# Two loops of a diffusion trunk: ScalarE copies each projection out of PSUM, VectorE works on the copies

## The chip, the cores and the metric

One NeuronCore of a Trainium2 chip runs the whole program. The metric is the device time of one execution in microseconds (us). Five engines work side by side: TensorE (PE, with its weight loads as PEld), VectorE (DVE), ScalarE (ACT), GpSimd (POOL) and SyncE (SP, which here only issues DMAs). Matrix products are written to PSUM; everything else lives in SBUF.

## The reference, cut to what matters

The program is one inference step of a trunk with two layers over 640 tokens (128 of context, 512 of latents) and a model width of 1024. In each layer four mixers run, and their outputs are gated, projected and merged. What the change touches is the end of a layer, in which the last branch's projection is merged and the output projection is added to the residual with a per-channel gate:

```
merged = pv + (1 + ttd) * (branch @ w_branch_out)   # last branch, per channel tile
x      = x + gate * (merged @ w_out)                # gate: one number per channel, one for latents, one for context
```

Here `pv` is the sum of the other three branches and `ttd` what the merge gate (a sigmoid, made from a tanh) needs for that branch; an earlier part of the kernel left both in device memory. After the second layer a last RMSNorm ends the trunk. All is float32.

## The kernel before, in words

Activations lie feature-major: a tile is 128 channels by 640 tokens, and the model width is 8 such tiles (`KD`). A float32 product is made of three TensorE products: each operand is split into a high part (a rounded copy, `hi`) and what is left (`lo = x - hi`), and `mm3` (lines 144 to 152) multiplies hi by hi (L148), weights' hi by activations' lo (L150) and weights' lo by activations' hi (L152). `split_to` (L128 to L131) makes the parts: ScalarE copies (L130), VectorE or POOL subtracts (L131). `w_chunk` (L133) loads a chunk of weights of 128 x 512 (`wraw`, by a DMA that SP issues) and splits it into `whi` and `wlo`; all three have two buffers. `fm_tile` (L154) makes one output tile: it takes a PSUM tile (tag `s`, two buffers), and for each chunk of weights runs four `mm3`.

Two loops at a layer's end are changed.

The **last branch's projection** (weights `wbo[l, 1]`, 8 tiles, one chunk each, 24 matmuls each). For each tile the PSUM result `bo` (traced as `s`) is read by VectorE in L1467, `ht = (ht + 1) * bo`, where `ht` has been loaded from `ttd`; L1468 adds `pv` (traced as `sq`), and `split_to` makes `hhi` and `hlo` (ScalarE L130, VectorE L131), which are the operands of the next loop. The split of the weights runs on ScalarE (`whi`) and POOL (`wlo`), as the last argument `G` says.

The **output projection** (weights `wout`, 8 tiles, two chunks each, 48 matmuls each). VectorE reads the PSUM result in L1477, twice a tile: once for the 512 latent tokens (a strided view of 2 x 256) and once for the 128 context tokens, since the gate `ga` differs, and adds the residual `xo` (also traced as `ht`). Then ScalarE squares the new tile and VectorE adds up the squares (`square_sum`, L252 to L261); in the last layer ScalarE also scales the tile by the last norm's weights.

In layer 0 both loops also carry steps of the next layer's state-space preparation: `preps(n)` takes `n` steps of a generator (tables `WPREPS` and `PREPS`, a number of steps for each tile). Its products `WY` and `WYt` come from VectorE (L462, and L464, which adds the two) and POOL (L463; later in the loop L513, L516 and L519 in the same manner); TensorE transposes the result (L449), ScalarE takes the transposes out of PSUM (L450, `Wt`) and issues the DMA that stores them (L452). In layer 1 there is nothing to prepare, and both loops stand alone.

TensorE runs its instructions in the order in which the code is written (`manual_schedule`). On the other engines, and on the DMA queues, a scheduler of the framework sets the order at build time, from the dependences and its own costs. So a change of the code can move instructions that it doesn't name.

Of the kernel before, what the change touches and what calls it, by code (L numbers as in the profile page):

```python
# [14 lines left out]
AF = mybir.ActivationFunctionType  # L15
ALU = mybir.AluOpType
AX = mybir.AxisListType

P = 128
# [3 lines left out]
NT = 640  # L23
# [32 lines left out]
def hybrid_kernel(ctx: ExitStack, tc: tile.TileContext, A, O, dbg=None):  # L56
    nc = tc.nc
    V, S, G, T = nc.vector, nc.scalar, nc.gpsimd, nc.tensor
# [12 lines left out]
    def taker(pool):  # L71
        def take(tag, shape, bufs=1, dt=F32):
            return pool.tile(shape, dt, tag=tag, name=nm(tag), bufs=bufs)
        return take
# [6 lines left out]
    def load(dst, src):  # L81
        nc.sync.dma_start(dst, src)
        return dst
# [44 lines left out]
    def split_to(hi, lo, src, eng=V):  # L128

        S.activation(hi, src, AF.Copy)  # L130
        eng.tensor_tensor(lo, src, f(hi), ALU.subtract)  # L131
# [22 lines left out]
    def fm_tile(src, mhi, mlo, nk=KD, eng=V):  # L154

        o = psum2()
        kc = min(nk, 4)
        for kq in range(nk // kc):
            w = w_chunk(src[kq], [P, kc, P], eng)
            for kk in range(kc):  # L160
                k = kq * kc + kk
                mm3([o[:, 0, 192:512], o[:, 1, 0:320]], w[0][:, kk], w[1][:, kk],
                    [mhi[:, k, 0:HF], mhi[:, k, HF:NT]], [mlo[:, k, 0:HF], mlo[:, k, HF:NT]], k == 0, k == nk - 1)
        return run2(o)[:, 192:832]
# [87 lines left out]
    def square_sum(at, acc, x, k, tag="sq", bufs=2, last=None):  # L252

        if k == 0:
            S.activation(acc, x, AF.Square)
        else:
            sq = at(tag, [P, NT], bufs)
            S.activation(sq, x, AF.Square)
            if k == last:
                return sq  # L260
            V.tensor_tensor(acc, acc, sq, ALU.add)  # L261
# [1025 lines left out]
    xat = taker(xp)  # L1287
    xt = xat("xt", [P, KD, NT])
# [5 lines left out]
    def preps(n):  # L1294

        for _ in range(n):
            next(prep, None)
# [4 lines left out]
    for l in range(DEPTH):  # L1302
# [10 lines left out]
        for k in range(KD):  # L1313
            sh, sc = mods[l, 0], mods[l, 1]
            t = xat("ht", [P, NT], 2)
# [137 lines left out]
        ga = mods[l, 2]  # L1453
# [5 lines left out]
        xat = taker(xp)  # L1459
# [3 lines left out]
        for d_ in range(KD):  # L1463
            bo = fm_tile(A["wbo"][l, 1, d_], *b, 4, G)
            t = load(xat("ht", [P, NT], 2), ttd[l][1][d_])
            pv = load(xat("sq", [P, NT], 2), mgd[l][2][d_])
            V.scalar_tensor_tensor(t, t, 1.0, bo, op0=ALU.add, op1=ALU.mult)  # L1467
            V.tensor_tensor(t, t, pv, ALU.add)  # L1468
            split_to(mhi[:, d_], mlo[:, d_], t)
            preps(WPREPS[d_])  # L1470
        xt = xat("xt", [P, KD, NT])
        acc = xat("acc", [P, NT])
        for d_ in range(KD):
            g = fm_tile(A["wout"][l, d_], mhi, mlo, KD, G)
            xo = load(xat("ht", [P, NT], 2), (A["xT"] if l == 0 else xd)[:, d_])
            for s_, v_ in ((0, samp), (1, lambda z: z[:, 256:384])):
                V.scalar_tensor_tensor(v_(xt[:, d_]), v_(g), ga[:, d_, s_:s_ + 1], v_(xo), op0=ALU.mult, op1=ALU.add)  # L1477
            if not last:
                nc.sync.dma_start(xd[:, d_], xt[:, d_])
            sq = square_sum(xat, acc, xt[:, d_], d_, last=KD - 1)  # L1480
            parts = [acc, sq]
            if last:
                S.activation(xt[:, d_], xt[:, d_], AF.Copy, scale=fnc[:, d_:d_ + 1])
            preps(PREPS[d_])
# [166 lines left out]
```

## Time and profile before

| | |
|---|---|
| median of 3 runs | 2310.57 us (2305.61 to 2311.26) |
| the profiled execution | 2309.3 us |
| its span | 2307.5 us |
| mean granted clock of TensorE | 0.961 |
| TensorE matmul busy | 2109.0 us, 91% |
| VectorE busy | 1375.3 us, 60% |
| ScalarE busy | 1031.0 us, 45% |
| POOL busy | 905.1 us, 39% |

Busy time is the time in which an engine runs an instruction, and the share is of the span. The span lies inside the execution's own time: here 1.8 us lie around it. These are averages over stages of different kinds, so they don't tell what limits the two loops; the rows further down are from those loops. They run twice: in layer 0 the first loop spans about 1115 to 1161 us and the second to 1238 us, in layer 1 the first spans about 2205 to 2234 us and the second to 2290 us.

### The profile page before, as it was taken

What the parts mean: (1) busy time and instruction counts of PE and PEld (TensorE: products, weight loads), DVE (VectorE), ACT (ScalarE), POOL (GpSimd) and SP (SyncE); (2) the same over time, 40 slices, a digit from 0 to 9 for tenths busy, and PEclk for the clock granted to TensorE, in tenths of its full rate; (3) what the DMA queues carried; (4) which work ended last, traced back from release to release, by engine and by line L of the source; (5) the groups of instructions that cost most, each with busy time, mean ns of one, the idle gap of its engine ahead of it and who ended that gap; (6) DMA issues with size and microseconds to landing.
All of it is one profiled execution on the core that took longest, in us unless ns stands there. A gap on an engine that the chain in (4) does not pass through costs nothing. (4 is left out here: it accounts for less than half of the span.)

```text
span 2307.5 us, 38266 instructions
## 1 busy us (share of the span) xinstructions
PE 2109.0 (91%) x14197; PEld 2010.3 (87%) x14197; DVE 1375.3 (60%) x2515; ACT 1031.0 (45%) x2069; POOL 905.1 (39%) x637
## 2 busy tenths in 40 slices
PE   5876889969999999998799999997999999999997
PEld 2876789969998889998788999897899899999997
DVE  7998672755455455665777685349345455565542
ACT  5332343314556665553233444341346656554332
POOL 4477431312335552345553364232132523234522
PEclk9988999989999999999899999998999999999998
DMA  6455576533745666666473386763384455566643
GB/s 219 118 189 200 183 240 189 175 90 120 214 140 152 179 193 181 182 196 198 155 252 129 117 249 217 248 180 93 102 249 131 148 149 156 174 188 184 201 148 116
DMA packets 238635, 400.60 MB, mean 174 GB/s; under 512 B 36400, under 2 KB 110128, under 8 KB 238448
## 3 DMA queue, kind: packets, MB, share of 16 engines
q1 hardware_dynamic: 224208, 372.13, 53.5%
q10 hardware_dynamic: 14240, 26.02, 3.1%
q8 instruction: 111, 1.82, 0.4%
q14 instruction: 76, 0.62, 0.1%
HBM read 279.67 MB, written 117.87 MB: 172 GB/s over the span
## 5 line engine op out<-in xcount | busy, mean ns | idle before, releaser
L131 POOL TENSOR_TENSOR flo<-fraw,fhi 128x512 fp32r<-128x512 f32 x368 | 528.4, 1443 | 897.4 <-ACT fhi L130 850.4
L148 PE MATMUL mm<-hhi,fhi 128*128 128x320 f32 x2048 | 667.2, 326 | 25.2 <-DVE gt L764 7.5
L152 PE MATMUL mm<-hhi,flo 128*128 128x320 f32 x2048 | 640.8, 313 | 7.0 <-POOL flo L131 7.0
L150 PE MATMUL mm<-hlo,fhi 128*128 128x320 f32 x2048 | 639.8, 312 | 0.0
L148 PEld LDWEIGHTS mm<-hhi,fhi 128*128 128x128 f32 x2048 | 393.7, 192 | 38.3 <-ACT rx L942 8.0
L152 PEld LDWEIGHTS mm<-hhi,flo 128*128 128x128 f32 x2048 | 391.2, 191 | 8.2 <-POOL flo L131 8.0
L150 PEld LDWEIGHTS mm<-hlo,fhi 128*128 128x128 f32 x2048 | 392.9, 192 | 0.8
L130 ACT ACTIVATE fhi<-fraw 128x512 fp32r<-128x512 f32 x368 | 228.2, 628 | 166.3 <-PE mm L150 102.7
L131 DVE TENSOR_TENSOR ptl<-sm,pth 128x512 fp32r<-128x512 f32 (+1 forms) x240 | 142.4, 621 | 166.0 <-ACT pth L130 165.7
L786 DVE TENSOR_REDUCE mx<-s 128x1 f32<-128x640 f32 (+1 forms) x240 | 167.4, 714 | 106.2 <-PE s L819 51.2
L131 POOL TENSOR_TENSOR wlo<-wraw,whi 128x512 fp32r<-128x512 f32 (+1 forms) x80 | 117.7, 1474 | 219.9 <-ACT whi L130 205.6
L130 ACT ACTIVATE pth<-sm 128x512 fp32r<-128x512 f32 (+1 forms) x240 | 122.2, 543 | 126.7 <-PE sm L846 97.6
L819 PE MATMUL s<-k,q 128*128 128x384 f32 (+5 forms) x1008 | 159.1, 305 | 2.6 <-ACT p L788 1.8
L819 PEld LDWEIGHTS s<-k,q 128*128 128x128 f32 (+1 forms) x1008 | 155.0, 189 | 3.5 <-ACT p L788 2.1
L130 ACT ACTIVATE whi<-wraw 128x512 fp32r<-128x512 f32 (+1 forms) x96 | 59.1, 617 | 168.1 <-PE s L150 88.2
L148 PE MATMUL mm<-bh,fhi 128*128 128x320 f32 x384 | 126.2, 329 | 5.5 <-DVE gt L764 3.6
L717 ACT ACTIVATE gt<-mm 128x320 f32<-128x320 f32 x192 | 83.0, 432 | 90.4 <-PE mm L152 88.7
L846 PE MATMUL sm<-ident,p 128*128 128x128 f32 x800 | 116.0, 274 | 7.9 <-DVE ptl L131 2.9
L869 PE MATMUL sm<-pth,v 128*128 128x256 f32 (+1 forms) x528 | 120.4, 282 | 0.3 <-ACT pth L130 0.3
L152 PE MATMUL mm<-bh,flo 128*128 128x320 f32 x384 | 119.8, 312 | 0.0
L150 PE MATMUL mm<-bl,fhi 128*128 128x320 f32 x384 | 119.8, 312 | 0.1
L869 PE MATMUL sm<-ptl,v 128*128 128x256 f32 (+1 forms) x440 | 112.6, 281 | 0.5 <-DVE ptl L131 0.5
(425 smaller groups left out, 4170.7 us busy)
## 6 DMA issues: line engine op xcount, KB each, us to landing
fraw<-in_wmerge SPq DMA_DIRECT2D x128, 256.0 KB, 3.0
fraw<-in_wgate SPq DMA_DIRECT2D x64, 256.0 KB, 2.9
fraw<-in_wmod SPq DMA_DIRECT2D x64, 256.0 KB, 2.8
mgd<-gt SPq DMA_DIRECT2D x48, 320.0 KB, 2.8
fraw<-in_wbo SPq DMA_DIRECT2D x48, 256.0 KB, 3.0
k<-dkd SPq DMA_DIRECT2D x64, 192.0 KB, 4.0
gtd<-gt SPq DMA_DIRECT2D x32, 320.0 KB, 3.3
pv<-mgd SPq DMA_DIRECT2D x32, 320.0 KB, 3.8
```

Source lines behind the costliest of these rows:

```text
L130: S.activation(hi, src, AF.Copy)
L131: eng.tensor_tensor(lo, src, f(hi), ALU.subtract)
L148: T.matmul(outs[i], lhsT=whi, rhs=mhis[i], start=first, stop=False)
L150: T.matmul(outs[i], lhsT=whi, rhs=mlos[i], start=False, stop=False)
L152: T.matmul(outs[i], lhsT=wlo, rhs=mhis[i], start=False, stop=last)
L717: S.activation(t[:, r[0]], r[1], AF.Tanh, scale=0.5)
L786: V.tensor_reduce(mx[:, 0:1], s, axis=AX.X, op=ALU.max, negate=True)
L819: T.matmul(o, lhsT=tok(q, t), rhs=k[:, a:b], start=i == 0, stop=i == n - 1)
L846: T.transpose(pt[:, a:a + P], p[:, jj, P * kt:P * kt + P], ident)
L869: T.matmul(o, lhsT=v, rhs=p_, start=n == 0, stop=n == len(todo) - 1)
```

## The change

In the first loop a new tile `ob` (128 x 640, two buffers) takes ScalarE's copy of the PSUM result, and VectorE's instruction reads `ob` in its place. In the second loop ScalarE multiplies the PSUM result by the gate while it copies (one instruction for the latents' view, one for the context), and VectorE adds the residual to the copy in one instruction over all 640 tokens, where there were two.

```diff
@@ -1464,7 +1464,9 @@
             bo = fm_tile(A["wbo"][l, 1, d_], *b, 4, G)
             t = load(xat("ht", [P, NT], 2), ttd[l][1][d_])
             pv = load(xat("sq", [P, NT], 2), mgd[l][2][d_])
-            V.scalar_tensor_tensor(t, t, 1.0, bo, op0=ALU.add, op1=ALU.mult)
+            ob = xat("ob", [P, NT], 2)
+            S.activation(ob, bo, AF.Copy)
+            V.scalar_tensor_tensor(t, t, 1.0, ob, op0=ALU.add, op1=ALU.mult)
             V.tensor_tensor(t, t, pv, ALU.add)
             split_to(mhi[:, d_], mlo[:, d_], t)
             preps(WPREPS[d_])
@@ -1473,8 +1475,10 @@
         for d_ in range(KD):
             g = fm_tile(A["wout"][l, d_], mhi, mlo, KD, G)
             xo = load(xat("ht", [P, NT], 2), (A["xT"] if l == 0 else xd)[:, d_])
+            ob = xat("ob", [P, NT], 2)
             for s_, v_ in ((0, samp), (1, lambda z: z[:, 256:384])):
-                V.scalar_tensor_tensor(v_(xt[:, d_]), v_(g), ga[:, d_, s_:s_ + 1], v_(xo), op0=ALU.mult, op1=ALU.add)
+                S.activation(v_(ob), v_(g), AF.Copy, scale=ga[:, d_, s_:s_ + 1])
+            V.tensor_tensor(xt[:, d_], ob, xo, ALU.add)
             if not last:
                 nc.sync.dma_start(xd[:, d_], xt[:, d_])
             sq = square_sum(xat, acc, xt[:, d_], d_, last=KD - 1)
```

In the changed kernel the copy of the first loop is line 1468, VectorE's two instructions are lines 1469 and 1470, the gated copies of the second loop are line 1480 and the addition is line 1481.

The scheduler places the new instructions, and moves others. Three places matter.

ScalarE in layer 1's first loop, before (`whi` is a weight chunk's high part, `hhi` a merged tile's high part):

```order
L130 ACTIVATE whi_24410<-wraw_24408 128x512
L130 ACTIVATE hhi_24286<-ht_24360 128x640
L130 ACTIVATE whi_24449<-wraw_24447 128x512
L130 ACTIVATE hhi_24286<-ht_24399 128x640
L130 ACTIVATE whi_24488<-wraw_24486 128x512
```

And in the changed kernel:

```order
L130 ACTIVATE whi_24407<-wraw_24405 128x512
L1468 ACTIVATE ob_24357<-s_24322 128x640
L130 ACTIVATE hhi_24318<-ht_24353 128x640
L130 ACTIVATE whi_24448<-wraw_24446 128x512
L1468 ACTIVATE ob_24398<-s_24363 128x640
L130 ACTIVATE hhi_24318<-ht_24394 128x640
L130 ACTIVATE whi_24489<-wraw_24487 128x512
```

The copy `ob` of a tile now stands between the weights' split for the tile two further on and the `hhi` of the same tile, which is made of what VectorE computes from that `ob`.

POOL in layer 0's first loop, before (`WYt` belongs to the preparation of the next layer, `wlo` is the low part of a weight chunk, here of tiles 2, 3 and 4 in that order):

```order
L463 TENSOR_TENSOR WYt_12565<-PW_6653,BX_12335 128x1024
L131 TENSOR_TENSOR wlo_12351<-wraw_12348,whi_12350 128x512
L463 TENSOR_TENSOR WYt_12692<-PW_6653,BX_12335 128x1024
L131 TENSOR_TENSOR wlo_12393<-wraw_12390,whi_12392 128x512
L463 TENSOR_TENSOR WYt_12711<-PW_6653,BX_12335 128x1024
L131 TENSOR_TENSOR wlo_12443<-wraw_12440,whi_12442 128x512
```

And in the changed kernel:

```order
L463 TENSOR_TENSOR WYt_12579<-PW_6653,BX_12339 128x1024
L131 TENSOR_TENSOR wlo_12355<-wraw_12352,whi_12354 128x512
L463 TENSOR_TENSOR WYt_12710<-PW_6653,BX_12339 128x1024
L463 TENSOR_TENSOR WYt_12729<-PW_6653,BX_12339 128x1024
L131 TENSOR_TENSOR wlo_12399<-wraw_12396,whi_12398 128x512
L131 TENSOR_TENSOR wlo_12451<-wraw_12448,whi_12450 128x512
```

Two of the preparation's products now stand ahead of the `wlo` of tile 3, where there was one.

ScalarE in layer 0's second loop, before (L258 squares a finished tile for the norm):

```order
L130 ACTIVATE whi_12849<-wraw_12847 128x512
L450 ACTIVATE Wt_12784<-sm_12785 128x512
L450 ACTIVATE Wt_12784<-sm_12791 128x512
L258 ACTIVATE sq_12781<-xt_12615 128x640
L452 DMA wtd_107<-Wt_12784 128x1024
```

And in the changed kernel:

```order
L130 ACTIVATE whi_12869<-wraw_12867 128x512
L1480 ACTIVATE ob_12796<-s_12733,mod_1234_6825 128x2x256
L1480 ACTIVATE ob_12796<-s_12733,mod_1234_6825 128x128
L450 ACTIVATE Wt_12804<-sm_12805 128x512
L450 ACTIVATE Wt_12804<-sm_12811 128x512
L452 DMA wtd_107<-Wt_12804 128x1024
```

The two gated copies stand ahead of the copies that take the preparation's transposes out of PSUM.

## Rows read from the trace of the kernel before

**Rows 1.** Stretches: start:end, length, busy us (count) by engine, PEclk, DMA share, GB/s.

```profile
1112.00:1140.00 28.00, 19.04 (x116) 18.31 (x114) 26.08 (x21) 6.32 (x11) 16.64 (x10) 0.88 0.45 141
1128.50:1132.00 3.50, 3.45 (x13) 3.48 (x14) 3.50 (x2) 0.00 (x0) 3.49 (x2) 0.50 0.08 30
1143.60:1149.20 5.60, 5.53 (x21) 5.56 (x22) 3.38 (x4) 0.74 (x1) 0.32 (x1) 0.50 0.70 220
2185.00:2291.00 106.00, 105.00 (x724) 104.91 (x722) 38.06 (x59) 36.41 (x57) 35.97 (x27) 1.00 0.43 135
```

**Rows 2.** Waits, 1112 to 1168 us: waiting, waited for, us, times, longest.

```profile
PE s L148 <- DVE ht L1467: 12.6, 3, 6.7
```

**Rows 3.** Timeline of PE in layer 0: start, duration, instruction, [idle before and its releaser].

```profile
1128.55 0.87 PE L148 MATMUL s<-bh,whi 128*128 128x320 f32 x2 [6.71 <-DVE ht L1467]
...
1143.67 0.87 PE L148 MATMUL s<-bh,whi 128*128 128x320 f32 x2 [5.23 <-DVE ht L1467]
...
1178.08 1.15 PE L449 MATMUL sm<-ident,WY 128*128 128x128 f32 x8 [0.25 <-ACT Wt L450]
...
1210.20 0.56 PE L152 MATMUL s<-hhi,wlo 128*128 128x320 f32 x2 [3.43 <-POOL wlo L131]
```

**Rows 4.** Timeline of DVE, layer 0 and an earlier stage of it.

```profile
677.31 1.89 DVE L774 SCALAR_TENSOR_TENSOR gl<-o,gl 128x640 f32<-128x640 f32 x1
...
1113.38 0.81 DVE L774 SCALAR_TENSOR_TENSOR gl<-o,gl 128x640 f32<-128x640 f32 x1
...
1125.40 2.27 DVE L464 TENSOR_TENSOR WY<-WY,WYt 128x1024 f32<-128x1024 f32 x1 [1.92 <-POOL WYt L463]
...
1142.72 0.81 DVE L1467 SCALAR_TENSOR_TENSOR ht<-ht,s 128x640 f32<-128x640 f32 x1
...
1165.77 0.83 DVE L131 TENSOR_TENSOR hlo<-ht,hhi 128x640 fp32r<-128x640 f32 x1 [0.81 <-ACT hhi L130]
```

**Rows 5.** Timeline of POOL, layer 0, the same stages.

```profile
677.23 1.29 POOL L131 TENSOR_TENSOR flo<-fraw,fhi 128x512 fp32r<-128x512 f32 x1 [4.73 <-ACT fhi L130]
...
1122.43 2.94 POOL L463 TENSOR_TENSOR WYt<-PW,BX 128x1024 f32<-128x1024 f32 x1 [3.43 <-DVE WY L464]
1125.33 1.26 POOL L131 TENSOR_TENSOR wlo<-wraw,whi 128x512 fp32r<-128x512 f32 x1
1127.75 2.03 POOL L463 TENSOR_TENSOR WYt<-PW,BX 128x1024 f32<-128x1024 f32 x1 [1.16 <-DVE WY L464]
...
1142.08 1.85 POOL L131 TENSOR_TENSOR wlo<-wraw,whi 128x512 fp32r<-128x512 f32 x1
```

**Rows 6.** Timeline of ACT: layer 0's first loop, then layer 1's first loop.

```profile
1144.64 0.74 ACT L130 ACTIVATE hhi<-ht 128x640 fp32r<-128x640 f32 x1 [4.91 <-DVE ht L1468]
...
2208.67 0.63 ACT L130 ACTIVATE whi<-wraw 128x512 fp32r<-128x512 f32 x1 [2.79 <-PE s L150]
...
2222.30 0.74 ACT L130 ACTIVATE hhi<-ht 128x640 fp32r<-128x640 f32 x1 [2.38 <-DVE ht L1468]
2222.94 0.62 ACT L130 ACTIVATE whi<-wraw 128x512 fp32r<-128x512 f32 x1
```

**Rows 7.** Timeline of POOL in layer 1's first loop.

```profile
2209.38 1.30 POOL L131 TENSOR_TENSOR wlo<-wraw,whi 128x512 fp32r<-128x512 f32 x1 [16.21 <-ACT whi L130]
...
2223.63 1.42 POOL L131 TENSOR_TENSOR wlo<-wraw,whi 128x512 fp32r<-128x512 f32 x1 [2.34 <-ACT whi L130]
```

**Rows 8.** Timeline of DVE in layer 1: first loop, then the second loop's first tile.

```profile
2224.66 1.07 DVE L1468 TENSOR_TENSOR ht<-ht,sq 128x640 f32<-128x640 f32 x1
...
2240.65 1.01 DVE L1477 SCALAR_TENSOR_TENSOR xt<-s,mod,ht 128x512 f32<-128x512 f32 x2 [2.88 <-PE s L152]
```

**Rows 9.** ScalarE's instructions nearest to the new ones, by source line and on its timeline.

```profile
L1310 ACT ACTIVATE R<-s x2: 704/704/704, 19.6 to 1245.9; 128x640 f32<-128x640 f32 x2
...
1250.86 1.01 ACT L1318 ACTIVATE hhi<-ht,mod 128x512 fp32r<-128x512 f32 x2 [0.26 <-DVE ht L1317]
```

**Rows 10.** Timeline of DVE and POOL at the end of layer 0's second loop.

```profile
1237.72 0.99 DVE L1477 SCALAR_TENSOR_TENSOR xt<-s,mod,ht 128x512 f32<-128x512 f32 x2
...
1237.73 2.26 POOL L516 TENSOR_TENSOR WYt<-PW,BX 128x1152 f32<-128x1152 f32 x1 [1.43 <-DVE WY L519]
```

## The prediction, made before the changed kernel was run

> **What bounds the kernel now.** I began with the stretches, since a share over the whole span says nothing of two short loops. In layer 1 (the last line of [rows 1]) TensorE is busy 105.00 of 106.00 us at clock 1.00, while VectorE and ScalarE work a third of the time: TensorE alone bounds that stretch. Its 724 matmuls take 0.145 us each, so a tile of the first loop (24 matmuls) takes 3.5 us and one of the second loop (48) 7.0. In the start of layer 0's first loop (the first line of [rows 1]) it is the other way: VectorE is busy 26.08 of 28.00 us and TensorE 19.04. The waits there [rows 2] name the instruction that the change edits: TensorE stood 12.6 us for L1467, 6.71 and 5.23 of them at two places [rows 3], because VectorE was busy with the preparation and left PSUM full. Behind both stops TensorE ran at clock 0.50, for 3.50 and 5.60 us [rows 1]; at the full clock half of that would do, so 4.5 us more belong to them. The price of VectorE's lateness is thus 12.6 + 4.5 = 17.1 us.
>
> The next view is the timeline of VectorE beside that of POOL, for a hold between the two. L774, a scalar_tensor_tensor with both operands in SBUF, takes 0.81 us alone, but 1.89 when POOL's split begins 0.08 ahead of it: it ends at 679.20, 0.68 after the split's end at 678.52 [rows 4, 5]. L464 at 1125.40 behaves the same (2.27). L1467 at 1142.72 has one operand in PSUM, runs inside a POOL split (1142.08 to 1143.93) and takes 0.81. So an instruction with two SBUF operands that meets a running POOL instruction ends some 0.68 after it, and one that reads PSUM isn't held. The change turns the second kind into the first.
>
> **Layer 1, first loop.** Added for each tile: ScalarE's copy, 0.70 us by the 128x640 copy from PSUM [rows 9]. ScalarE's order closes a ring: `whi` of tile d+2, `ob` of tile d, then `hhi` of tile d, which waits for VectorE's pair on that `ob`, and only then the next `whi`. POOL's `wlo` starts 0.69 after its `whi` (2222.94 to 2223.63) and ends 2.11 after it, at 2225.05 [rows 6, 7]. VectorE is ready for `ob` at about 0.64 + 0.70 + 0.04 = 1.38, inside the `wlo`, so L1469 is held and ends 0.68 after it. The sum L1470 adds 0.85 (1.07 with its own hold in [rows 8], less 0.22), the semaphore 0.04, and from `hhi` to the next `whi` 0.64 (2222.30 to 2222.94). The ring is 2.11 + 0.68 + 0.85 + 0.04 + 0.64 = 4.32 us a tile, over TensorE's 3.5.
>
> It starts where it did, with the `whi` at 2208.67 and the `wlo` ending 2210.68: L1469 ends 2211.36, L1470 2212.21, the next `whi` starts 2212.89. Six more turns bring that to 2238.8; 3.68 later the last `hhi` starts, at 2242.5, and `hlo` ends 1.6 later (0.74 + 0.04 + 0.83, the last from [rows 4]), at 2244.1. Four matmuls end the second loop's first tile 0.6 later, at 2244.7; now it ends at 2240.65, where L1477 starts [rows 8]. That is **+4.1**. Bounds: 0 if nothing is held (0.64 + 0.70 + 0.04 + 0.81 + 0.85 + 0.04 + 0.64 = 3.72 a tile then, 1.4 at most, part of it hidden), +4.9 if each turn costs a further 0.1.
>
> On VectorE's price for an SBUF operand: 0.81 alone with both operands in SBUF, 0.81 with one in PSUM [rows 4], no difference, so I take none. The Trainium skill (Perfetto Trace Analysis, section Optimizing Scalar/DVE Operations) puts VectorE's overhead at about 60 ns on SBUF and 125 on PSUM. By it the ring would lose 0.065, the seven turns 0.5 and the sum would be 2315.2; the trace decides, and no row here shows that gain.
>
> **Layer 0, first loop.** The copies empty PSUM early, so the 12.6 us of waiting for L1467 go. What is late next is POOL. Tile 2's `wlo` ends at 1126.59 (1125.33 + 1.26), two us before TensorE now starts the tile. Tile 3's `wlo` now stands behind two `WYt`. The first starts at 1127.7, where the next one starts now, and takes 2 to 3 us [rows 5]; the second waits until VectorE has used the first (1.2 to 2.3 [rows 4]) and takes the same. That puts the `wlo`'s end at about 1137. So TensorE stops once more, now for POOL and near half clock after it, ends tile 3 at about 1141.6 and starts tile 4 two us before the present 1143.67. From there the ring runs as in layer 1. By the same steps tile 2's `hhi` starts at 1146.8 (now 1144.64 [rows 6]); five turns of 4.3 and the `hlo` bring tile 7's `hlo` to about 1169.3, where it ends at 1166.60 now [rows 4]. TensorE's reserve at tile 4 is thus lost in the ring, and the second loop's first tile ends **+1.8** later. Bounds: -4.4 if the ring runs at 3.7, +3 if `WYt` and the ring hold each other.
>
> **Layer 0, second loop.** The gated copies (1.01 for the pair of 2 x 256; of the context's 128 I count only what the tails below do) stand ahead of the `Wt` copies, for which TensorE's next transposes wait (0.25 at 1178.08 [rows 3]). Where they meet that is 0.4 to 0.8; I take four places at 0.4, +1.6. Behind them stands a wait of 3.43 for a `wlo` at 1210.20 [rows 3]: it takes up 1.8 + 1.6 = 3.4, if POOL keeps its time. So layer 0's two loops come to **0** (-7 to +5).
>
> **The two tails.** The last tile's epilogue is open in each layer. Before: VectorE's pair, 1.01 [rows 8]. After: ScalarE's pair, 1.01 by the like pair L1318 [rows 9], 0.04, then an addition of 0.82: +0.86. In layer 1 that is **+0.9**. In layer 0 a POOL instruction of 2.26 us starts beside it [rows 10], and the addition, with two SBUF operands, can be held up to 2; I take **+1.4**. What the change removes from VectorE (16 instructions of the second loop) is worth nothing: in [rows 8] VectorE had waited 2.88 us for TensorE.
>
> **Sum.** 0 + 1.4 + 4.1 + 0.9 = +6.4 on the profiled execution's 2309.3: **2315.7**. That execution lies 1.3 below the median of the runs, 2310.57. A difference of 0.3% (6.9 us) is about what a measurement of this kernel can tell from no change: 2303.6 to 2317.5 is "the same".
>
> **The rivals.** *Slower still.* POOL in layer 0's second loop takes its next `WYt` from VectorE, whose order runs them behind the last `hlo`. If that chain starts late, the `wlo` that TensorE awaits at 1210.20 is late too, and absorbs nothing: 3.4 us more, and 1.6 if the transposes lose 0.8 each. 6.4 + 5 gives 2320.7. It decides from the point where POOL's `wlo` there ends after 1212. For: the order now has two `WYt` ahead of a `wlo` in a row. Against: the 3.43 us wait has POOL, not VectorE, as its releaser.
>
> *The port goes to VectorE first.* If L1469 starts ahead of the `wlo`, POOL is held instead and the ring is 3.72: layer 1 +1, layer 0 -4.4, tails +1.7, 2307.6. Against: `wlo` starts 0.69 after `whi`, the copy is ready at 1.38.
>
> *Faster.* VectorE is the saturated engine in layer 0, and all that was lost to it is gained: 17.1 - 6.4 = 10.7 less, 2298.6. It needs tile 3's `wlo` to end before 1132 and the second loop's `wlo` to come earlier as well. The same section of the Trainium skill says that where VectorE is saturated, giving work to ScalarE may pay. Against: VectorE's instructions stay what they are in this loop, its 26.08 us are not lightened, and `wlo` is late next.
>
> *Nothing happens.* The copies hide, the ring is not the bound because `whi` is made ahead, and the scheduler's other moves cancel: 2309.
>
> **How the numbers follow.** Forecast (+3 to +9): 0.51, of which 0.31 is the same and 0.20 slower by over 0.3%, as its middle lies 1.8 below the edge. Slower still: 0.25. Port: 0.11 (0.10 the same). Faster: 0.09. Nothing: 0.04. Together: faster 0.10, the same 0.45, slower 0.45. The range must reach from the port case with layer 0's lower bound to the slower rival with a bound of 3 on its parts: 2303 to 2324; the forecast's own is 2312 to 2318.
>
> **What would show it.** In the profile after: in layer 1's first loop L1469 lasting 1.2 to 1.4 us and ending 0.68 after a `wlo`, `whi` starting every 4.3 us, TensorE waiting for `hhi` or `hlo` at the start of the second loop, L1481 first starting near 2245.5. In layer 0 no wait for L1469, but one of about 5 us for `wlo` in tile 3, and `hlo` of tile 7 near 1169. I am wrong if `whi` comes every 3.5 us in layer 1, or if TensorE's waits in layer 0's first loop sum to under 3 us, or if stages outside these loops differ by more than 2 us.

## The result, and the profile after

The changed kernel takes 2322.66 us in the median of 4 runs (2319.67 to 2324.58), the kernel before 2309.01 beside it (4 runs, 2305.61 to 2311.26). The ratio is 1.0059 with a 95% interval of 1.0041 to 1.0077: slower. The interval leaves out 1, and the difference is twice the 0.3% that the prediction took for the least that can be told from no change. The profiled execution spans 2320.1 us where the one before spans 2307.5.

To find the place, I cut both spans at the same instructions: VectorE's L774 ahead of each layer's first loop, the last `hlo` of the first loop, TensorE's first matmul on the last square (L268), ScalarE's copy of the norm's factors `R` at the start of the next layer, and VectorE's first final multiplication. Times in us:

| | before | after |
|---|---|---|
| start to L774 of layer 0 | 1113.4 | 1113.9 |
| L774 to the end of layer 0's last `hlo` | 53.2 | 56.0 |
| L774 to the last square | 126.2 | 135.1 |
| L774 to `R` | 132.5 | 143.0 |
| `R` to L774 of layer 1 | 954.0 | 951.2 |
| L774 of layer 1 to the final multiplications | 97.8 | 102.1 |
| from there to the end | 9.8 | 9.8 |

So 10.5 us come from the end of layer 0, most of them in its second loop, and 4.3 from the end of layer 1. The stretch between, which the change does not touch, is 2.8 shorter; a second profile of the kernel before has 951.3 there (experiment 6), so a difference of this size comes without the change.

First layer 1. ScalarE, POOL and VectorE over one turn of the first loop after the change (timelines; the columns are those of [rows 3]):

```profile
2220.53 0.74 ACT L130 ACTIVATE hhi<-ht 128x640 fp32r<-128x640 f32 x1 [2.36 <-DVE ht L1470]
2221.18 0.61 ACT L130 ACTIVATE whi<-wraw 128x512 fp32r<-128x512 f32 x1
2221.69 0.68 ACT L1468 ACTIVATE ob<-s 128x640 f32<-128x640 f32 x1
2224.86 0.74 ACT L130 ACTIVATE hhi<-ht 128x640 fp32r<-128x640 f32 x1 [2.49 <-DVE ht L1470]
2225.51 0.62 ACT L130 ACTIVATE whi<-wraw 128x512 fp32r<-128x512 f32 x1
...
2221.87 1.42 POOL L131 TENSOR_TENSOR wlo<-wraw,whi 128x512 fp32r<-128x512 f32 x1 [2.91 <-ACT whi L130]
...
2222.41 1.56 DVE L1469 SCALAR_TENSOR_TENSOR ht<-ht,ob 128x640 f32<-128x640 f32 x1 [0.28 <-ACT ob L1468]
2224.01 0.82 DVE L1470 TENSOR_TENSOR ht<-ht,sq 128x640 f32<-128x640 f32 x1
```

From `whi` to `whi` it is 4.33 us, where [rows 6] show `hhi` and `whi` alone. POOL's `wlo` ends at 2223.29, L1469 at 2223.97, 0.68 later: the hold of [rows 4, 5], in a stretch where VectorE works a third of the time [rows 1]. ScalarE stands 2.4 us in each turn for VectorE's pair, and TensorE, which set the pace before, now follows the ring: it runs 215 matmuls from 2216.0 to 2250.7, 34.7 us, where before it ran 240 in 35.0 (2205.0 to 2240.0).

Next layer 0's first loop, where TensorE had waited 12.6 us for L1467 [rows 2]. The lines show its two long waits for POOL now, in tiles 2 and 3, then the second of the two `WYt` that stand ahead of the `wlo` of tile 3, and the last `hlo`:

```profile
1127.18 0.64 PE L152 MATMUL s<-bh,wlo 128*128 128x320 f32 x1 [4.14 <-POOL wlo L131]
...
1137.40 0.64 PE L152 MATMUL s<-bh,wlo 128*128 128x320 f32 x1 [3.78 <-POOL wlo L131]
...
1133.13 2.54 POOL L463 TENSOR_TENSOR WYt<-PW,BX 128x1024 f32<-128x1024 f32 x1 [1.89 <-DVE WY L464]
1135.64 1.71 POOL L131 TENSOR_TENSOR wlo<-wraw,whi 128x512 fp32r<-128x512 f32 x1
...
1169.14 0.83 DVE L131 TENSOR_TENSOR hlo<-ht,hhi 128x640 fp32r<-128x640 f32 x1 [0.80 <-ACT hhi L130]
```

The wait for VectorE is gone, and 7.9 us of waiting for POOL have come; the ring, 4.3 us a tile here too (`whi` starts at 1147.56, 1151.88 and 1156.22), does the rest.

Layer 0's second loop. What ScalarE, VectorE, POOL and TensorE did around the third tile's addition:

```profile
1201.13 0.74 ACT L258 ACTIVATE sq<-xt 128x640 f32<-128x640 f32 x1 [7.53 <-DVE xt L1481]
1201.77 1.13 ACT L130 ACTIVATE whi<-wraw 128x512 fp32r<-128x512 f32 x2
1202.81 0.92 ACT L1480 ACTIVATE ob<-s,mod 128x512 f32<-128x512 f32 x2
1203.63 1.08 ACT L450 ACTIVATE Wt<-sm 128x512 f32<-128x512 f32 x2
...
1196.33 0.69 DVE L476 TENSOR_SCALAR BX<-BX 128x1024 f32<-128x1024 f32 x1 [2.85 <-DMA BX<-in_Cri]
1196.94 1.35 DVE L513 TENSOR_TENSOR WY<-PW,BX 128x1152 f32<-128x1152 f32 x1
1198.21 2.89 DVE L1481 TENSOR_TENSOR xt<-ob,ht 128x640 f32<-128x640 f32 x1
...
1197.15 3.25 POOL L516 TENSOR_TENSOR WYt<-PW,BX 128x1152 f32<-128x1152 f32 x1 [2.52 <-DVE BX L476]
...
1204.27 0.33 PE L449 MATMUL sm<-ident,WY 128*128 128x128 f32 x1 [4.11 <-ACT Wt L450]
```

Read from the last line back: TensorE's transposes wait 4.11 us for `Wt`; ScalarE made no `Wt` because it stood in front of a square for 7.53; the square needs L1481, which took 2.89 beside POOL's L516 and, in VectorE's new order, stands behind L476, which waits for a DMA. From 1165 to 1262 us TensorE's waits for `wlo` fell from 3.9 us to 1.3, but those for `Wt` rose from 1.4 to 6.0.

The costliest groups of VectorE from 1113 to 1262 us (count, then busy us and mean ns) give the sum of such holds, after and before:

```profile
L1469 DVE SCALAR_TENSOR_TENSOR ht<-ht,ob 128x640 f32<-128x640 f32 x8 | 15.2, 1905 | 0.3 <-DMA ht<-ttd 0.3
L1481 DVE TENSOR_TENSOR xt<-ob,ht 128x640 f32<-128x640 f32 x8 | 14.4, 1800 | 5.0 <-ACT ob L1480 4.9
```

```profile
L1467 DVE SCALAR_TENSOR_TENSOR ht<-ht,s 128x640 f32<-128x640 f32 x8 | 6.5, 812 | 0.2
L1477 DVE SCALAR_TENSOR_TENSOR xt<-s,mod,ht 128x512 f32<-128x512 f32 x8 | 5.9, 743 | 7.0 <-PE s L152 4.8 <-DMA ht<-in_xT 2.1
L1477 DVE SCALAR_TENSOR_TENSOR xt<-s,mod,ht 128x128 f32<-128x128 f32 x8 | 2.7, 338 | 0.0
```

The change was to take work off VectorE; in layer 0 it added 8.7 us to VectorE's busy time in the first loop and 14.4 - 8.6 = 5.8 in the second.

At the end of layer 0 the last addition is held (1.97) by the POOL instruction that the prediction named in [rows 10], and TensorE waits 3.88 us for the last square, where it waited 1.92:

```profile
1246.18 1.97 DVE L1481 TENSOR_TENSOR xt<-ob,ht 128x640 f32<-128x640 f32 x1 [0.91 <-ACT ob L1480]
...
1245.21 2.25 POOL L516 TENSOR_TENSOR WYt<-PW,BX 128x1152 f32<-128x1152 f32 x1 [1.42 <-DVE WY L519]
...
1248.97 0.27 PE L268 MATMUL sm<-ones,sq 128*128 128x1 f32 x1 [3.88 <-ACT sq L258]
```

### The profile page after: what moved, and what is told of

Read it like the earlier page. It is cut to its first block, busy times and chain, and to the rows that moved or that the text cites. A ratio compares the mean times of both kernels' runs of the same rounds, so it can differ in the third digit from the quotient of the medians.

```text
span 2320.1 us, 38288 instructions
## 1 busy us (share of the span) xinstructions
PE 2115.2 (91%) x14197; PEld 2011.4 (87%) x14197; DVE 1390.9 (60%) x2499; ACT 1051.4 (45%) x2117; POOL 909.2 (39%) x637
## 5 line engine op out<-in xcount | busy, mean ns | idle before, releaser
L869 PE MATMUL sm<-pth,v 128*128 128x256 f32 (+1 forms) x528 | 121.1, 283 | 0.6 <-ACT pth L130 0.6
```

The lines of the kernel that those rows point to most:

```text
L869: T.matmul(o, lhsT=v, rhs=p_, start=n == 0, stop=n == len(todo) - 1)
```

## The experiments

My theory after this reading: the ring and the holds in both loops, with the order of VectorE's queue in layer 0's second loop as a cost of its own. The rivals are that the loss is a matter of order alone, or that a late first loop pushes the second. Marks below are counted from L774 as in the table.

**1. The first loop's copies alone** (the second loop's lines as before).

> The copies of the first loop alone, the second loop as before. Theory (the ring of ScalarE and VectorE costs 4.3 us a tile, and what it delays in layer 0 is partly taken up by the wait of 3.4 us for wlo in the second loop): ring at 4.3 us a tile in both layers, layer 1 from the last L774 to the final multiplications 101 to 102 us (97.8 before), layer 0 from L774 at its first loop to the next layer's R 132 to 135.5 us (132.5 before), in all +4 to +7 us. Rival A (a late first loop pushes POOL's whole chain of the second loop and nothing is taken up): layer 0 at 138 us or more, in all +9 or more. Rival B (the first loop's copies cost nothing, everything lies in the second loop): in all within 2 us of before.

Measured: 2313.53 us against 2309.13, ratio 1.0021 (1.0010 to 1.0031). Layer 0 has its `R` at 136.7 (132.5), layer 1 takes 101.3 (97.8), the ring 4.3. The total is within the theory's bounds, but layer 0 is a miss, between the theory's and rival A's numbers: nothing was taken up. The marks of the two layers add up to 7.7 us, more than the 4.4 by which the runs differ; what gives the rest back isn't shown (this profile's stretch between the layers, 944.9, is the shortest of all). TensorE's wait for `wlo` in the second loop is as long as in [rows 3]; it only comes later:

```profile
1217.20 0.63 PE L152 MATMUL s<-hhi,wlo 128*128 128x320 f32 x1 [3.43 <-POOL wlo L131]
```

The kernel before shows why it moves along. The pair of `wlo` that TensorE awaits there stands behind POOL's L516, and L516 had itself waited 5.55 us for VectorE's chain:

```profile
1205.54 2.27 POOL L516 TENSOR_TENSOR WYt<-PW,BX 128x1152 f32<-128x1152 f32 x1 [5.55 <-DVE WY L519]
1207.76 4.20 POOL L131 TENSOR_TENSOR wlo<-wraw,whi 128x512 fp32r<-128x512 f32 x2
```

**2. The second loop's gated copies alone** (the first loop's lines as before).

> The gated copies of the second loop alone, the first loop as before. Theory (VectorE's new order puts L476, which waits for a DMA, ahead of the addition of tile 2; ScalarE's square of that tile waits in front of the copies that TensorE's transposes need; and the last tile's addition is held by POOL): a wait of 3 to 4 us for Wt at the fourth set of transposes, a wait of 3.5 to 4 us for the last square, clock near 0.6 behind it, layer 0 +4 to +8 us, layer 1 +0 to +1, in all +4 to +9. Rival A (these waits come only because the first loop is late): layer 0 within 2 us of before.

Measured: 2322.48 us, ratio 1.0059 (1.0040 to 1.0078), as much as the whole change. The last `hlo` is where it was (53.6), `R` at 145.1 is 12.6 later, and layer 1 takes 99.6 (97.8). All three are more than the theory's bounds (+4 to +9 in all, +4 to +8 in layer 0, up to +1 in layer 1): it had the place right and the price too low. The waits named are there without any lateness of the first loop, so rival A falls:

```profile
1202.20 0.47 PE L449 MATMUL sm<-ident,WY 128*128 128x128 f32 x1 [4.45 <-ACT Wt L450]
...
1250.11 0.37 PE L268 MATMUL sm<-ones,sq 128*128 128x1 f32 x1 [3.89 <-ACT sq L258]
```

The parts don't add up (4.4 and 13.3 against 13.6). Most of the overlap lies in layer 0, where they lose 4.2 and 12.6 and the whole change 10.5: what the first loop loses there, the second loop loses anyway.

**3. Tile 2 of layer 0's second loop as before**, which in VectorE's order puts it ahead of L476:

```diff
-            ob = xat("ob", [P, NT], 2)
...
+            if l or d_ != 2:
+                ob = xat("ob", [P, NT], 2)
...
+            else:
+                for s_, v_ in ((0, samp), (1, lambda z: z[:, 256:384])):
+                    V.scalar_tensor_tensor(v_(xt[:, d_]), v_(g), ga[:, d_, s_:s_ + 1], v_(xo), op0=ALU.mult, op1=ALU.add)
```

> The whole change, but tile 2 of layer 0's second loop as before: VectorE reads PSUM, and its order then has tile 2 ahead of L476. Theory (that order is what made TensorE wait 4.1 us for Wt at 1204): that wait falls below 1 us, layer 0 is 1 to 4 us shorter than with the whole change. Rival (the gated copies ahead of the Wt copies are the cause): the wait stays at 3 us or more, as tile 3 still has its gated copies there.

Measured: 2322.29 us, ratio 1.0060 (1.0039 to 1.0081), no gain; layer 0 has its `R` at 144.5 (143.0), not 1 to 4 us earlier. The wait of 4.11 fell to 0.92, as the theory had it, and TensorE waited for `wlo` instead:

```profile
1203.58 0.33 PE L449 MATMUL sm<-ident,WY 128*128 128x128 f32 x1 [0.92 <-ACT Wt L450]
...
1216.64 0.42 PE L152 MATMUL s<-hhi,wlo 128*128 128x320 f32 x1 [1.60 <-POOL wlo L131]
...
1230.13 0.42 PE L152 MATMUL s<-hhi,wlo 128*128 128x320 f32 x1 [2.67 <-POOL wlo L131]
```

The order made that wait, but did not make the loss. POOL's `wlo` stands between the preparation's products, and these take turns with VectorE; that chain was late whatever order the third tile had. Its last addition L519 ends 131.8 us after L774, against 131.2 with the whole change and 124.3 before.

**4. The last tile of the second loop as before**, in both layers (the same `if`, with `d_ < KD - 1`).

> The whole change, but the last tile of the second loop as before in both layers. Theory (the last addition is held by POOL's L516, the square comes 2 us later, and TensorE's clock falls in the longer wait): layer 0's wait for the last square falls from 3.9 to about 1.9 us, the granted clock in the 8 us behind it rises from 0.62 to about 0.8, layer 0 is 3 to 4 us shorter than with the whole change, layer 1 0.5 to 1 us, in all 3 to 5 us. Rival (the late preparation on VectorE sets the end, not the addition): the wait stays above 3 us and the time within 1 us of the whole change.

Measured: 2317.70 us, ratio 1.0042 (1.0025 to 1.0058), an interval that overlaps that of the whole change. The wait for the last square fell to 1.76 and layer 1 to 101.5, as expected. The clock did not come back: 0.57 in the 8 us behind the square, as with the whole change. Layer 0 was not 3 to 4 us shorter but 1.8 longer, with `R` at 144.8, in this profile, the slowest of the seven runs, in which L476 waited 4.40 us for its DMA (2.85 with the whole change). What the tail is worth in layer 0 isn't settled by this run.

**5. The copies written back to PSUM.** ScalarE does the same work, but VectorE's instruction has one operand in PSUM again (against the whole change; the two lines that make `ob` go as well):

```diff
-            S.activation(ob, bo, AF.Copy)
-            V.scalar_tensor_tensor(t, t, 1.0, ob, op0=ALU.add, op1=ALU.mult)
+            S.activation(bo, bo, AF.Copy)
+            V.scalar_tensor_tensor(t, t, 1.0, bo, op0=ALU.add, op1=ALU.mult)
...
-                S.activation(v_(ob), v_(g), AF.Copy, scale=ga[:, d_, s_:s_ + 1])
-            V.tensor_tensor(xt[:, d_], ob, xo, ALU.add)
+                S.activation(v_(g), v_(g), AF.Copy, scale=ga[:, d_, s_:s_ + 1])
+            V.tensor_tensor(xt[:, d_], g, xo, ALU.add)
```

> The whole change, but ScalarE writes its copy and its gated product back to the same PSUM tile, and VectorE reads them there: ScalarE's work and nearly all the order stay, VectorE's instruction has one operand in PSUM again, and the PSUM tile stays taken until VectorE has read it. Theory (the holds between VectorE's two-SBUF instructions and POOL are the price): in layer 1's first loop VectorE's instruction takes 0.8 us in place of 1.53 and the ring 3.5 to 3.75 us a tile, layer 1 from the last L774 to the final multiplications 98 to 99.7 us (102.1 with the whole change); in layer 0 the preparation's chain on VectorE and POOL ends its last addition L519 within 126 us of L774 (124.2 before, 131.2 with the whole change), and R comes before 139 us (132.5 and 143.0). Rival (ScalarE's place in the ring and the order of the queues are the price, whoever reads what): ring still 4.3, layer 0 at 141 us or more.

Measured: 2305.63 us against 2307.01, ratio 0.9993 (0.9980 to 1.0005): the loss is gone from the total, with the copies still on ScalarE. L476 still stands ahead of the third tile's addition and still waits for its DMA. One turn of the first loop in layer 1, then that addition in layer 0 beside POOL's L516:

```profile
2211.22 0.62 ACT L130 ACTIVATE whi<-wraw 128x512 fp32r<-128x512 f32 x1
2211.75 0.69 ACT L1467 ACTIVATE s<-s 128x640 f32<-128x640 f32 x1
2214.18 0.74 ACT L130 ACTIVATE hhi<-ht 128x640 fp32r<-128x640 f32 x1 [1.75 <-DVE ht L1469]
2214.82 0.62 ACT L130 ACTIVATE whi<-wraw 128x512 fp32r<-128x512 f32 x1
...
2211.92 1.42 POOL L131 TENSOR_TENSOR wlo<-wraw,whi 128x512 fp32r<-128x512 f32 x1 [2.30 <-ACT whi L130]
...
2212.46 0.82 DVE L1468 SCALAR_TENSOR_TENSOR ht<-ht,s 128x640 f32<-128x640 f32 x1 [0.29 <-ACT s L1467]
...
1192.10 0.82 DVE L1479 TENSOR_TENSOR xt<-s,ht 128x640 f32<-128x640 f32 x1
...
1191.05 3.28 POOL L516 TENSOR_TENSOR WYt<-PW,BX 128x1152 f32<-128x1152 f32 x1 [2.58 <-DVE BX L476]
```

The ring is 3.60 us. VectorE's instruction starts inside the `wlo` as before and takes 0.82; in layer 0 the third addition takes 0.82 in the midst of a POOL instruction, where it took 2.89. The preparation's chain ends at 121.1 (124.3 before, 131.2 after), the last `hlo` at 50.9, `R` at 131.8; layer 1 takes 99.7. So layer 1 still loses 1.9 of the 4.3 (the ring is over TensorE's 3.5, and the wait for the last square is 2.64, 1.75 before), and layer 0, which ends a little earlier than before, makes up for it. The rival, with its 4.3 and 141, falls. One thing changes besides: the PSUM tile is free only when VectorE has read it. The trace shows the price: in layer 0's first loop TensorE waits 10.6 us for VectorE's L1468 (12.6 for L1467 before) and not for POOL. The wait that the copy was to remove is back.

**6. The kernel before once more.**

> The kernel before once more, for how far the marks of one profile move from run to run: from L774 to R in layer 0 132.5 us in the first profile, the stretch between the two layers' marks 954.0, layer 1 97.8. If the marks of layer 0 and 1 move by less than 1 us, differences of 3 us and more between kernels can be read from single profiles, and the stretch between, which was 945 to 954 in all kernels, is what varies. If they move by 3 us or more, they can't.

Measured: 2305.3 us in its profiled execution. Last `hlo` at 54.1 (53.2), last square at 125.9 (126.2), `R` at 133.8 (132.5), the stretch between 951.3 (954.0), layer 1 97.9 (97.8). The marks of the loops move by up to 1.3 us and the stretch between by 2.7. Over the twelve profiles of this case the start up to L774 of layer 0 takes 1110.5 to 1117.1 us and the stretch between 944.9 to 954.0, neither in any order with the change; so it is the marks that can be compared from profile to profile, not the spans. From the last square to `R`, 6.4 us before and 8.0 after the change, this second profile of before has 8.0 too, behind a wait of 1.92, with a granted clock of 0.57 in the 8 us behind the square (0.79 in the first profile): that difference, which I had put down to a lower clock after a longer wait, comes and goes in one and the same kernel.

**7. The plain copies for tiles 0 to 2 of layer 0's first loop alone.**

> The kernel before with the plain copies for tiles 0 to 2 of layer 0's first loop alone, where TensorE waited 12.6 us for VectorE. Theory (wlo of tile 3, behind two WYt, is late next, but the ring is broken from tile 3 on): TensorE waits 7 to 9 us for wlo in tiles 2 and 3 instead, the last hlo of layer 0 ends 1 to 3 us earlier than before, and the whole is -3 to +1 us. Rival (the relief of VectorE is real and was eaten by the ring alone): 8 us or more faster.

Measured: 2309.93 us against 2307.01, ratio 1.0001 (0.9988 to 1.0013). No difference from before can be told; the ratio lies within the theory's bounds, the medians, 2.9 apart, do not. TensorE waited 3.78 and 4.89 us for `wlo`, the sum foreseen, but the last `hlo` was not early (55.0), as a wait of 3.66 us for VectorE's L1472, the product of a tile without a copy, came at tile 5. The rival falls: PSUM emptied early is worth nothing where POOL's `wlo` is next. What a relief of VectorE is worth the run doesn't show, as the three products on copies are held themselves (2.66, 1.88 and 1.48 us, where 0.81 was usual).

**8. The low part of the weights by VectorE in layer 1's first loop**, copies in SBUF (the last argument of `fm_tile` is `V if last else G`).

> The whole change, but the low part of the weights in layer 1's first loop is made by VectorE in place of POOL; the copies stay in SBUF. Theory (what holds L1469 is a POOL instruction that runs beside it, not where its operand lies): without one, L1469 takes 0.82 us in place of 1.53 though both its operands lie in SBUF; VectorE then has 0.7 us more of its own a tile, some of it ahead of L1469, so the ring is 3.6 to 4.3 us. Rival (an instruction with two SBUF operands is slower here for another reason, a port that ScalarE or the DMAs take): L1469 stays at 1.4 us or more.

Measured, in a single execution of 2317.74 us: layer 1 takes 99.8 us (102.1 with the whole change). Without a POOL instruction beside it L1469, with both its operands in SBUF, takes 0.82; the turns that start as in the order of the whole change are 3.82:

```profile
2219.68 0.69 DVE L131 TENSOR_TENSOR wlo<-wraw,whi 128x512 fp32r<-128x512 f32 x1
2220.28 0.82 DVE L1469 SCALAR_TENSOR_TENSOR ht<-ht,ob 128x640 f32<-128x640 f32 x1
2221.13 0.83 DVE L1470 TENSOR_TENSOR ht<-ht,sq 128x640 f32<-128x640 f32 x1
```

So in this loop it is neither the place of the operands nor POOL alone that costs, but the two together.

**9. Copies in PSUM in layer 0 alone, its last tile as before.**

> Copies written back to PSUM in layer 0 alone, the last tile of its second loop as before; layer 1 as before. Theory (without the holds the copies relieve VectorE and TensorE in layer 0: the last hlo 2 to 3 us earlier, and nothing of it is lost in the tail or in layer 1): layer 0 from L774 to R 130 to 131.5 us (132.5 and 133.8 in the two profiles of before), layer 1 97.8, in all 1 to 4 us faster than before. Rival (the preparation's chain sets the end of layer 0, whatever the loops do): within 1 us of before.

Measured: 2306.66 us, ratio 0.9991 (0.9977 to 1.0005). `R` at 130.2, layer 1 98.7. Layer 0 ends earlier than in any other kernel, where the theory had it; the total can't be told from before. TensorE is not relieved, though the theory had that too: it waits 11.0 us for VectorE in layer 0's first loop.

**10. Copies in PSUM in layer 0's first loop alone.**

> Copies written back to PSUM in layer 0's first loop alone, all else as before. Theory: last hlo 2 to 3 us earlier than before (51 us after L774 against 53 to 54), and the second loop, with its old order, keeps 1 to 3 us of it: in all 1 to 3 us faster. Rival (the wait of 3.4 us for wlo in the second loop takes it all): within 1 us of before.

Measured: 2302.88 us against 2308.11, ratio 0.9983 (0.9968 to 0.9998), the one version whose interval lies below 1, by little; one such interval among eight versions is weak evidence. The last `hlo` is at 50.6, 2.6 to 3.5 earlier, the last square at 125.5, 0.3 to 0.7 earlier, and `R` at 131.9, 0.6 to 1.9 earlier: most of the gain is lost in the second loop.

## Why the prediction came out as it did

The measured 2322.66 lies in the range (2303 to 2324), on the side that was forecast as likely as no change, but it is nearest to the rival called slower still (2320.7), not to the forecast (2315.7). That it lies inside is in part luck: one of the four runs (2324.58) does not, and the holds of layer 0's additions ahead of the tail were in neither sum. Step by step:

- **Layer 1: right.** The ring was priced at 4.32 us and is 4.33, held as foreseen, with L1469 ending 0.68 after `wlo`. L1469 lasts 1.43 to 1.56 us and not 1.2 to 1.4, as the copy is ready a little sooner; its end, and so the ring, stays with the `wlo`. The two terms, 4.1 and 0.9, make 5.0; layer 1 lost 4.3. Experiments 5 and 8 show the cause by taking away one half of the conflict each. The 0.68 is that of a 128x640 instruction: L464, which the prediction says behaves the same, ended 1.08 after the POOL instruction (1127.67 against 1126.59 [rows 4, 5]).
- **Layer 0, first loop: right but for one wait.** The wait for L1467 went, POOL was late next (tile 3's `wlo` ended at 1137.35, forecast 1137), and the last `hlo` ended at 1169.97, forecast 1169.3. The wait in tile 3 was 3.78 us, forecast about 5, and another of 4.14 came in tile 2: the prediction held that tile's `wlo` against the start that TensorE had before, 1128.55, which was itself late. The Trainium skill (SBUF — State Buffer, section Who interferes with whom) says that a VectorE instruction with two SBUF inputs contends with a GpSimd instruction that reads SBUF, and calls the contention an exclusive lock on the port pair that the two share. The trace agrees: 0.68 us of L1469 lie behind the `wlo`'s end, nearly all of the 0.82 that it takes without a POOL instruction beside it.
- **Layer 0, second loop: wrong, and nearly the whole miss.** I set it at 0: 1.8 and 1.6 of lateness, taken up by the wait of 3.43 for `wlo`, "if POOL keeps its time". Experiment 1 shows that POOL does not: with the first loop late the wait stayed 3.43 and layer 0 ended 4.2 later. And I priced the hold of the additions only in the last tile, as [rows 8], from layer 1, had VectorE idle there. In layer 0 the same eight additions stand between the preparation's instructions, where POOL is busy 39.56 of 64 us (1172 to 1236): 14.4 us in place of 8.6. Experiment 2 shows that the second loop's copies alone cost as much as the whole change, experiment 5 that without these holds layer 0 loses nothing. The bound of +5 for the two loops was too small as well: of layer 0's 10.5, 2.8 stood at the last `hlo`, 4.1 came in the second loop, 2.0 in the tail, and 1.6 behind the last square, which experiment 6 shows without the change. The 1.01 us that this step reads as a pair for the latents is one instruction for the latents and one for the context; nothing hung on it.
- **The tails: about right in size.** Forecast +1.4 and +0.9. The wait for the last square grew by 2.0 in layer 0 and by 0.8 in layer 1. The addition held by L516 was the right place.
- **The sum.** +6.4 was forecast and the span grew by 12.6. The stretch between the layers takes 2.8 off it; by the prediction's own list that is a sign of being wrong (over 2 us outside the loops), but experiment 6 shows as much without the change. The loops and tails gave 10.5 + 4.3 = 14.8, 8.4 more than forecast, nearly all of it in layer 0. The deciding point of the rival called slower still held: the `wlo` that TensorE awaited at 1210.20 had ended at 1210.14, and the one at the same place in POOL's order now ends at 1214.05, after 1212. Its mechanism came only in part. A chain that starts late does push the `wlo` (experiment 1), but in experiment 2 the first loop is on time and layer 0 loses still more, as the holds lengthen the chain itself. What spoke against it, that the wait's releaser was POOL and not VectorE, was no argument: POOL's own chain hung on VectorE.
- The rival in which the port goes to VectorE first did not come: each `wlo` of layer 1's first loop starts ahead of L1469. Nor did the faster one: no stretch of layer 0 ended earlier.

## What to carry to other kernels

Before moving a PSUM operand of VectorE to SBUF, look at POOL in the same stretch: an instruction that was not held becomes one that waits for a POOL instruction already running, and the price here was that of the hold, not of the copy. If ScalarE must help, it can write back to PSUM; here that avoided the holds, but it freed no PSUM early, so the wait that the copy was meant to remove stayed. And a wait further down absorbs lateness only if what it waits for does not move along: follow the releaser's own chain back before you count on it.

## What the runs showed of the hardware beyond this

L475, a tensor_scalar on one SBUF tile with a factor per partition, takes 0.74 us when it starts ahead of POOL's `WYt` (before; the `WYt` at 1139.65 took 2.46, where two others there took 2.03) and 2.51 when it starts inside one (after, with a `WYt` from 1133.13 to 1135.67):

```profile
1139.50 0.74 DVE L475 TENSOR_SCALAR BX<-BX,sgn 128x1024 f32<-128x1024 f32 x1
...
1133.71 2.51 DVE L475 TENSOR_SCALAR BX<-BX,sgn 128x1024 f32<-128x1024 f32 x1
```

So an instruction with a single large SBUF operand can be held as well. When it isn't held it is the faster kind: 0.74 us for 128x1024, where L464 with two operands takes 1.21. And the two gated copies of a tile, latents and context, took 0.64 and 0.34 us in layer 1 when ScalarE wrote to PSUM (experiment 5) and 0.67 and 0.36 when it wrote to SBUF; into PSUM the second started only when the first had ended, so the pair took 1.02 us there and 0.93 into SBUF. The plain copy took 0.69 either way.
